# Summing the exponentials over the keys with products by a column of ones in an encoder block on one core

## The chip, the cores and the metric

The kernel runs on one core of a Trainium2 chip. The metric is the device time of one execution in microseconds. TensorE is called PE in the profile (PEld is its weight load), VectorE is DVE, ScalarE is ACT, GpSimd is POOL and SyncE is SP.

## What is computed

One layer of an encoder over 2064 tokens (16 meta tokens ahead of 2048) of width 1024, all in float32: an input projection, attention of four query heads over two key and value heads beside a Fourier mixing, an output projection, and a feed-forward part with a squared relu. The part that the change touches is the attention:

```python
def attend(qb):
    s = jnp.einsum('bkgqd,bksd->bkgqs', qb, kt).astype(jnp.float32) * scale
    p = jax.nn.softmax(s, axis=-1).astype(vt.dtype)
    return jnp.einsum('bkgqs,bksd->bkgqd', p, vt)
```

The softmax needs, for every query, the largest score and the sum of the exponentials over all 2064 keys.

## The kernel before

Most products of matrices are made three times on halves of a float32 number that `split` makes (a rounded high part on ACT by line 68, the rest on DVE by line 69), by `mm3` (lines 78 to 80).

The attention works in 16 units: eight blocks of 256 tokens by two key heads. A unit has 512 columns, two query heads of 256 tokens each, and keys lie on the partitions. `scores` (line 736) makes the scores of 128 keys by 512 queries, ACT copies them out of PSUM (line 754), and DVE keeps a running maximum `M` over tiles of keys (line 760). `stats` (line 780) then makes one maximum per query of what is left on 128 partitions, spreads it over all partitions and copies it to `mb`. `softmax` (line 786) subtracts `mb` (DVE, line 813), takes exponentials (ACT, line 814), adds them to `acc` (DVE, line 820) and multiplies them with the values into `O`. At its end `sum` (lines 799 to 801) holds 128 partial sums for each of the 512 queries, one per partition. `finish` (line 832) adds these up over the partitions, takes the reciprocal `rl` (line 837), spreads it over the partitions by four transposes (`rows_to_cols`, line 773, product `pd_l` on line 777), and DVE multiplies `O` with it (line 840).

The step over the partitions is `over_keys` (line 764), used for the maximum and for the sum: four transposes of 128 by 128 into a PSUM bank `pm`, and one reduction on DVE from that bank into `mx`. `pm` and the bank `pd` of `rows_to_cols` share one PSUM bank: `misc` (line 681) has one buffer. So the sequence around the end of a unit is a chain through that bank: `pm_m` (PE), `mx_m` (DVE), `pd_m` (PE), `mb` (ACT) for the next unit's maximum, then `pm_l` (PE), `mx_l` (DVE), `rl` (DVE), `pd_l` (PE) for the sum of the unit that ends.

The scores of the next unit, the softmax of this one and other work are issued step by step through generators: the end of the Fourier part, then `out_f` (line 879), then the output projection and the feed-forward part of the blocks whose attention is done. The order in which instructions end up on each engine is set by a scheduler, so a change in one step can move others. Two more places have a product by the column `ones` (line 176): line 904, one product per token tile (`pys`), and line 979, four products in a row per block (`pas`).

Of the kernel before, what the change touches and what calls it, by code (L numbers as in the profile page):

```python
# [11 lines left out]
F32 = mybir.dt.float32  # L12
R32 = mybir.dt.float32r
AF = mybir.ActivationFunctionType
ALU = mybir.AluOpType
AX = mybir.AxisListType
# [3 lines left out]
P = 128  # L20
# [34 lines left out]
def f32v(ap):  # L55
    return ap.bitcast(F32)
# [30 lines left out]
def bc(ap, shape):  # L87
    return ap.broadcast_to(shape)
# [45 lines left out]
def encoder_block(ctx: ExitStack, tc: tile.TileContext, x, meta, w_in, w_f,  # L134
                  w_out, w_up, w_down, g_fin, g_cols, g_rows, c_id, c_rope, c_dft, c_even, c_odd, c_rem, out):
    nc = tc.nc
    split = Split(nc)
    x = x[0]
# [37 lines left out]
    ones = const.tile([P, 1], F32, name="ones", tag="ones")  # L176
# [402 lines left out]
    for j in range(LAST + 1):  # L579
# [16 lines left out]
        else:  # L596
# [14 lines left out]
            a = 0  # L611
# [67 lines left out]
    ap2 = Lines(tc.alloc_tile_pool(name="ap2", bufs=1, side="right", reuse_waits="tile"), small)  # L679

    def misc(name, shape=(P, 512)):
        return app.tile(list(shape), F32, name=name, tag="misc")
# [35 lines left out]
    def attention():  # L718
# [42 lines left out]
            if i == NT - 1:  # L761
                nc.vector.tensor_tensor(M[:, 0], M[:, 0], M[:, 1], op=ALU.max)

        def over_keys(x, name, op):

            ps = misc("pm_" + name, (P, 4, P))
            for a in range(4):
                nc.tensor.transpose(ps[:, a], x[:, a * P:(a + 1) * P], ident)
            r = ap2.tile([P, 4], F32, name="mx_" + name, tag="mx", bufs=2)
            nc.vector.tensor_reduce(r, ps, axis=AX.X, op=op)  # L770
            return r

        def rows_to_cols(vec, name):

            ps = misc("pd_" + name, (P, 4, P))
            for a in range(4):
                nc.tensor.transpose(ps[:, a], bc(vec[:, a:a + 1], [P, P]), ident)
            return ps.rearrange("p a e -> p (a e)")

        def stats(u):  # L780
            s = state[u]
            pd = rows_to_cols(over_keys(s["M"], f"m{u}", ALU.max), f"m{u}")
            mb = s["mb"] = ap2.tile([P, 512], F32, name=f"mb_{u}", tag="mb", bufs=1)
            nc.scalar.copy(mb, pd)  # L784

# [46 lines left out]
        def finish(u):  # L832
            b, g = units[u]
            s = state.pop(u)
            sl = over_keys(s["sum"], f"l{u}", ALU.add)
            rl = ap2.tile([P, 4], F32, name=f"rl_{u}", tag="rl", bufs=2)
            nc.vector.reciprocal(rl, sl)
            O = ap2.tile([P, 512], F32, name=f"O_{u}", tag="Osb", bufs=1)
            nc.scalar.copy(O, s["O"])
            nc.vector.tensor_tensor(O, O, rows_to_cols(rl, f"l{u}"), op=ALU.mult)  # L840
            c = slice(b % 2 * 256, b % 2 * 256 + 256)
            hi = ap2.tile([P, 512], R32, name=f"oh_{u}", tag="ph", bufs=2)
            lo = ap2.tile([P, 512], R32, name=f"ol_{u}", tag="pl", bufs=2)
            split(hi, lo, O)
            for e, t in enumerate((hi, lo)):
                nc.sync.dma_start(o_d[b // 2][:, e, 2 * g:2 * g + 2, c], f32v(t).rearrange("p (h n) -> p h n", h=2))
            nc.scalar.square(O, O)
            first = b not in sqs
            if first:
                sqs[b] = ap2.tile([P, 256], F32, name=f"sq_{b}", tag="sq", bufs=3)  # L850
                nc.vector.tensor_tensor(sqs[b], O[:, :256], O[:, 256:], op=ALU.add)
            else:
                for h in range(2):
                    nc.vector.tensor_tensor(sqs[b], sqs[b], O[:, h * 256:(h + 1) * 256], op=ALU.add)

        start(0)
        for i in range(NT + 1):
            scores(0, i)
        yield
        stats(0)  # L860
        for u in range(len(units)):
            nx = u + 1 < len(units)
            for i in range(NT + 1 + LAG):
                if i == 1 and nx:
                    start(u + 1)
                if i <= NT:
                    softmax(u, i)
                if nx and i >= LAG:
                    scores(u + 1, i - LAG)
                yield  # L870
            if nx:
                stats(u + 1)
            finish(u)
            yield
# [41 lines left out]
    class Att:  # L916
        def __init__(self):
            self.gen = attention()
            self.n = 0
            self.cap = 1 << 30  # L920
# [372 lines left out]
    sl = Lines(tc.alloc_tile_pool(name="sl", bufs=1, reuse_waits="tile"), small)  # L1293
# [46 lines left out]
    for g in range(8):  # L1340
# [5 lines left out]
        for name in ORDER:  # L1346
            hi, lo = ready.pop(0)
            m = BF[name]
            for p in range(2):
# [5 lines left out]
                ps = slice(p * P, (p + 1) * P)  # L1355
# [10 lines left out]
            for p in range(2):  # L1366
# [12 lines left out]
                else:  # L1379
                    q, a, b = {"2": ("11", Y, p1), "7": ("22", X, p5), "3": ("12", Y, u2)}[name]  # L1380
# [315 lines left out]
```

## Time and profile before

| | |
|---|---|
| median of 3 runs | 2306.72 us (2306.57 to 2309.46) |
| profiled execution, its own time | 2308.2 us |
| its span | 2306.4 us |
| PE busy | 2277.9 us (99%) |
| PE weight loads | 1879.5 us (81%) |
| DVE busy | 1713.4 us (74%) |
| ACT busy | 1295.7 us (56%) |
| granted clock of PE | 1.00 |

Busy time of PE counts from the start of a product to the modelled end of its results, and neighbouring products overlap; so the cost of a product in a full stream is read from the distance between starts. Times in the timeline are from the start of the span. A row "x4" merges four neighbouring instructions.

### The profile page before, as it was taken

To read this page: it belongs to the slowest core of one execution; us is meant where nothing else is said; L and a number is where in the kernel's file an instruction comes from. 1 tells how busy PE (TensorE), PEld (TensorE's weight loads), DVE (VectorE), ACT (ScalarE), POOL (GpSimd) and SP (SyncE) were. 2 spreads that over 40 slices of the span, in tenths; PEclk is the share of its full clock that TensorE was granted. 3 is DMA by queue.
4 is the path that set the end of the run, shared out by engine and by line. 5 is a ranking of instruction groups with operands and counts; after the bars stand their busy time and mean duration, and the time that the engine had idled before them with its cause. 6 is when DMAs were issued, how large, how long until landed. Compare 5 with 4: busy or idle time off the path is not lost.

```text
span 2306.4 us, 29992 instructions
## 1 busy us (share of the span) xinstructions
PE 2277.9 (99%) x10822; PEld 1879.5 (81%) x10822; DVE 1713.4 (74%) x2435; ACT 1295.7 (56%) x2335; POOL 204.2 (9%) x243
## 2 busy tenths in 40 slices
PE   8999999999999999999999999999999999999998
PEld 7888987777788888888878878888888888888887
DVE  6445578999887876976887976886675646697786
ACT  6443355666675665665775675664555555543344
POOL 1212120233100000000000100000100000200000
PEclk9999999999999999999999999999999999999999
DMA  6343252543533322343242453325344444855442
GB/s 209 101 119 97 83 154 74 174 147 114 192 102 100 103 87 78 110 121 106 97 161 68 151 189 106 98 80 187 120 156 171 149 161 147 311 193 165 129 137 83
DMA packets 178069, 307.23 MB, mean 133 GB/s; under 512 B 14960, under 2 KB 63728, under 8 KB 177536
## 3 DMA queue, kind: packets, MB, share of 16 engines
q1 hardware_dynamic: 159280, 263.16, 34.8%
q0 software_dynamic: 18640, 42.16, 6.1%
q8 instruction: 85, 1.39, 0.2%
q14 instruction: 64, 0.52, 0.1%
HBM read 225.27 MB, written 79.99 MB: 132 GB/s over the span
## 4 chain that ended last, share of the span: by engine, by line
PE 73%; DVE 1%; ACT 1%; issue 1%; POOL 0%; DMA 0%; POOLq 0%; DVEq 0%; ACTq 0%; SPq 0%
PE pdn L78 5%; PE pdn L79 5%; PE pdn L80 5%; PE pup L78 5%; PE pup L80 5%; PE pup L79 5%; PE dx L80 2%; PE dx L79 2%; PE dx L78 2%; PE ux L78 2%; PE ux L79 2%; PE ux L80 2%; PE o L78 2%; PE o L79 2%; PE o L80 2%; PE dy L80 2%
## 5 line engine op out<-in xcount | busy, mean ns | idle before, releaser
L78 PE MATMUL pup<-mT,wh_up 128*128 128x512 f32 x512 | 200.8, 393 | 0.7 <-ACT mT L71 0.7
L80 PE MATMUL pup<-mT,wl_up 128*128 128x512 f32 x512 | 200.8, 393 | 0.3 <-DVE wl_up L69 0.3
L79 PE MATMUL pup<-mT,wh_up 128*128 128x512 f32 x512 | 200.7, 392 | 0.0
L79 PE MATMUL pdn<-wl_dn,ah 128*128 128x512 f32 x512 | 200.5, 392 | 0.0
L78 PE MATMUL pdn<-wh_dn,ah 128*128 128x512 f32 x512 | 200.4, 393 | 0.0
L80 PE MATMUL pdn<-wh_dn,al 128*128 128x512 f32 x512 | 199.2, 391 | 0.0
L754 ACT COPY S<-s 128x512 f32<-128x512 f32 x256 | 148.8, 584 | 46.1 <-PE s L80 36.9
L68 ACT CAST wh_up<-wr_up 128x512 fp32r<-128x512 f32 x128 | 79.3, 621 | 159.2 <-PE pup L79 79.2
L813 DVE TENSOR_TENSOR S<-S,mb 128x1024 f32<-128x1024 f32 x128 | 156.6, 1233 | 10.0 <-ACT mb L784 9.9
L69 DVE TENSOR_TENSOR pl<-S,ph 128x512 fp32r<-128x512 f32 x196 | 133.6, 700 | 11.5 <-ACT ph L68 10.9
L69 DVE TENSOR_TENSOR wl_up<-wr_up,wh_up 128x512 fp32r<-128x512 f32 x128 | 87.4, 688 | 68.1 <-ACT wh_up L68 63.1
L814 ACT ACTIVATE S<-S 128x1024 f32<-128x1024 f32 x114 | 120.4, 1058 | 30.2 <-DVE S L813 29.9
L68 ACT CAST ph<-S 128x512 fp32r<-128x512 f32 x196 | 119.9, 621 | 30.7 <-PE o L80 26.9
L820 DVE TENSOR_TENSOR acc<-acc,S 128x1024 f32<-128x1024 f32 x110 | 134.9, 1226 | 0.8 <-ACT S L814 0.5
L68 ACT CAST wh_dn<-wr_dn 128x512 fp32r<-128x512 f32 x128 | 78.9, 619 | 98.0 <-PE pdn L80 47.3
L760 DVE TENSOR_TENSOR M<-M,S 128x1024 f32<-128x1024 f32 x96 | 118.3, 1233 | 15.9 <-ACT S L754 15.0
L69 DVE TENSOR_TENSOR wl_dn<-wr_dn,wh_dn 128x512 fp32r<-128x512 f32 x128 | 87.3, 689 | 51.2 <-ACT wh_dn L68 43.9
L68 ACT CAST ah<-a 128x1024 fp32r<-128x1024 f32 x56 | 58.5, 1048 | 117.7 <-issue 60.8
L78 PE MATMUL s<-q,kt 128*128 128x512 f32 (+1 forms) x272 | 113.2, 416 | 2.9 <-ACT S L754 1.8
L78 PEld LDWEIGHTS pdn<-wh_dn,ah 128*128 128x128 f32 x512 | 96.1, 188 | 22.3 <-ACT r L1088 1.9
L78 PEld LDWEIGHTS pup<-mT,wh_up 128*128 128x128 f32 x512 | 96.2, 188 | 20.3 <-ACT mT L71 0.9
L80 PEld LDWEIGHTS pup<-mT,wl_up 128*128 128x128 f32 x512 | 96.2, 188 | 19.9 <-DVE wl_up L69 0.8
(336 smaller groups left out, 6434.1 us busy)
## 6 DMA issues: line engine op xcount, KB each, us to landing
wr_up<-in_w_up_dram SPq DMA_DIRECT2D x128, 256.0 KB, 2.8
wr_dn<-in_w_down_dram SPq DMA_DIRECT2D x128, 256.0 KB, 2.6
a<-s_d SPq DMA_DIRECT2D x42, 512.0 KB, 3.7
R<-in_w_up_dram SPq DMA_DIRECT2D x16, 1024.0 KB, 5.3
s_d<-s SPq DMA_DIRECT2D x64, 256.0 KB, 2.1
d<-in_w_down_dram SPq DMA_DIRECT2D x26, 512.0 KB, 5.0
s_d<-c SPq DMA_DIRECT2D x48, 256.0 KB, 2.0
x<-in_x_dram SPq DMA_DIRECT2D x16, 512.0 KB, 4.8
```

The source lines that it names most:

```text
L68: self.high = nc.scalar.copy(hi, src)
L69: self.low = nc.vector.tensor_tensor(lo, src, f32v(hi), op=ALU.subtract)
L78: nc.tensor.matmul(out, a[0], b[0], start=first, stop=False, skip_group_check=chain)
L79: nc.tensor.matmul(out, a[0], b[1], start=False, stop=False, skip_group_check=chain)
L80: nc.tensor.matmul(out, a[1], b[0], start=False, stop=last, skip_group_check=chain)
L754: nc.scalar.copy(S[:, i % 2], ps)
L760: nc.vector.tensor_tensor(M, M, S, op=ALU.max)
L813: nc.vector.tensor_tensor(S, S, mb, op=ALU.subtract)
L814: nc.scalar.activation(p, S, AF.Exp, scale=ISQ)
L820: nc.vector.tensor_tensor(acc, acc, p, op=ALU.add)
```

## The change

The sum over the partitions is taken out of the shared helper. The helper keeps the maximum, with one buffer of `mx` in place of two. The sum is made by four products of PE: a block of 128 partitions by 128 queries of `sum` with the column of ones, each giving one column of a PSUM tile of 128 by 4. No reduction follows: the reciprocal reads the PSUM tile. Lines from 775 on have a number that is higher by 7 (the reciprocal, line 837, is line 844; `pd_l`, line 777, is line 784).

```diff
-        def over_keys(x, name, op):
+        def most_over_keys(x, name):
             ps = misc("pm_" + name, (P, 4, P))
             for a in range(4):
                 nc.tensor.transpose(ps[:, a], x[:, a * P:(a + 1) * P], ident)
-            r = ap2.tile([P, 4], F32, name="mx_" + name, tag="mx", bufs=2)
-            nc.vector.tensor_reduce(r, ps, axis=AX.X, op=op)
+            r = ap2.tile([P, 4], F32, name="mx_" + name, tag="mx", bufs=1)
+            nc.vector.tensor_reduce(r, ps, axis=AX.X, op=ALU.max)
             return r
+
+        def sum_over_keys(x, name):
+            ps = misc("pm_" + name, (P, 4))
+            for a in range(4):
+                nc.tensor.matmul(ps[:, a:a + 1], x[:, a * P:(a + 1) * P], ones, start=True, stop=True)
+            return ps
...
-            pd = rows_to_cols(over_keys(s["M"], f"m{u}", ALU.max), f"m{u}")
+            pd = rows_to_cols(most_over_keys(s["M"], f"m{u}"), f"m{u}")
...
-            sl = over_keys(s["sum"], f"l{u}", ALU.add)
+            sl = sum_over_keys(s["sum"], f"l{u}")
             rl = ap2.tile([P, 4], F32, name=f"rl_{u}", tag="rl", bufs=2)
             nc.vector.reciprocal(rl, sl)
```

Where it moves instructions is shown at three places. The first is PE at the end of unit 6 (units count from 0; `pup` are products of the feed-forward part), before:

```order
L768 MATMUL pm_l_8324<-ident,sum_8224 128x128 x4
L80 MATMUL pup_3_3_8241<-mT_0_6452,wl_up_3_3_8353 128x512
L78 MATMUL pup_3_0_8238<-mT_0_6452,wh_up_3_4_8374 128x512
L79 MATMUL pup_3_0_8238<-mT_0_6453,wh_up_3_4_8374 128x512
L80 MATMUL pup_3_0_8238<-mT_0_6452,wl_up_3_4_8375 128x512
L78 MATMUL pup_3_1_8239<-mT_0_6452,wh_up_3_4_8374 128x512
L79 MATMUL pup_3_1_8239<-mT_0_6453,wh_up_3_4_8374 128x512
L80 MATMUL pup_3_1_8239<-mT_0_6452,wl_up_3_4_8375 128x512
L78 MATMUL pup_3_2_8240<-mT_0_6452,wh_up_3_4_8374 128x512
L79 MATMUL pup_3_2_8240<-mT_0_6453,wh_up_3_4_8374 128x512
L777 MATMUL pd_l_8335<-ident,rl_8331 128x128 x4
```

The same place of PE in the changed kernel:

```order
L777 MATMUL pm_l_8312<-ones,sum_8212 128x1 x4
L80 MATMUL pup_3_3_8229<-mT_0_6444,wl_up_3_3_8339 128x512
L78 MATMUL pup_3_0_8226<-mT_0_6444,wh_up_3_4_8360 128x512
L79 MATMUL pup_3_0_8226<-mT_0_6445,wh_up_3_4_8360 128x512
L80 MATMUL pup_3_0_8226<-mT_0_6444,wl_up_3_4_8361 128x512
L78 MATMUL pup_3_1_8227<-mT_0_6444,wh_up_3_4_8360 128x512
L784 MATMUL pd_l_8321<-ident,rl_8317 128x128 x4
```

The spreading transposes `pd_l` stood nine products behind `pm_l` and stand five behind it now. Over the 16 units the distance was 8 to 13 products and is 2 to 9; it is three in units 1, 11 and 13, two in the last, and five or more in the others.

The second place is DVE at the end of the same unit, before:

```order
L770 TENSOR_REDUCE mx_m_8315<-pm_m_8310 128x4
L813 TENSOR_TENSOR S_0_7686<-S_0_7686,mb_8322 128x1024
L770 TENSOR_REDUCE mx_l_8329<-pm_l_8324 128x4
L69 TENSOR_TENSOR wl_up_3_7_8433<-wr_up_3_7_8430,wh_up_3_7_8432 128x512
L837 RECIPROCAL rl_8331<-mx_l_8329 128x4
L813 TENSOR_TENSOR S_2_7758<-S_2_7758,mb_8322 128x1024
```

DVE there in the changed kernel:

```order
L770 TENSOR_REDUCE mx_m_8303<-pm_m_8298 128x4
L820 TENSOR_TENSOR S_0_7674<-S_0_7674,mb_8310 128x1024
L844 RECIPROCAL rl_8317<-pm_l_8312 128x4
L69 TENSOR_TENSOR wl_up_3_7_8419<-wr_up_3_7_8416,wh_up_3_7_8418 128x512
L820 TENSOR_TENSOR S_2_7746<-S_2_7746,mb_8310 128x1024
```

The reduction is gone, and the reciprocal stands in its place, right behind the first subtraction of the next unit.

The third place is DVE at the end of unit 11 in the changed kernel (`h` are sums of the feed-forward part):

```order
L770 TENSOR_REDUCE mx_m_12337<-pm_m_12332 128x4
L69 TENSOR_TENSOR wl_dn_1_1_2_12463<-wr_dn_1_1_2_12460,wh_dn_1_1_2_12462 128x512
L1121 TENSOR_TENSOR h_0_9318<-h_0_9318,pdn_1_0_0_12260 128x512
L1121 TENSOR_TENSOR h_1_9320<-h_1_9320,pdn_1_0_1_12261 128x512
L844 RECIPROCAL rl_12351<-pm_l_12346 128x4
L820 TENSOR_TENSOR S_0_11684<-S_0_11684,mb_12344 128x1024
```

Here, and in units 1 and 13, the reciprocal stands ahead of the first subtraction of the next unit; before, the subtraction stood ahead of `mx_l` in all units but the last.

## Rows read from the trace of the kernel before

**Rows 1.** The page, busy time of each engine.

```profile
PE 2277.9 (99%) x10822; PEld 1879.5 (81%) x10822; DVE 1713.4 (74%) x2435; ACT 1295.7 (56%) x2335; POOL 204.2 (9%) x243
```

**Rows 2.** Stretches of the attention: busy us (and instructions) of each engine, granted clock.

```profile
403.00:581.00 178.00, 171.94 (x785) 132.49 (x784) 167.93 (x235) 108.71 (x205) 56.75 (x54) 1.00 0.44 145
581.00:665.00 84.00, 82.54 (x388) 66.70 (x387) 67.67 (x100) 56.02 (x105) 10.54 (x12) 1.00 0.49 158
665.00:1600.00 935.00, 934.43 (x4216) 762.65 (x4215) 743.39 (x1024) 596.08 (x1018) 35.02 (x46) 1.00 0.36 113
```

**Rows 3.** Who waited for whom on PE: us in total, times, longest.

```profile
PE o L79 <- DVE pl L69: 3.5, 5, 1.6
PE s L78 <- ACT S L754: 1.8, 2, 1.5
...
PE pof L80 <- DVE yl L69: 1.0, 3, 0.4
```

**Rows 4.** Timeline of PE at the end of unit 6: start, us.

```profile
837.39 0.40 PE L79 MATMUL pup<-mT,wh_up 128*128 128x512 f32 x1
837.63 0.60 PE L768 MATMUL pm_l<-ident,sum 128*128 128x128 f32 x4
837.98 0.48 PE L80 MATMUL pup<-mT,wl_up 128*128 128x512 f32 x1
838.30 0.40 PE L78 MATMUL pup<-mT,wh_up 128*128 128x512 f32 x1
838.53 0.40 PE L79 MATMUL pup<-mT,wh_up 128*128 128x512 f32 x1
...
840.17 0.62 PE L777 MATMUL pd_l<-ident,rl 128*128 128x128 f32 x4
```

**Rows 5.** Groups by line and form on PE: count, busy us, mean ns.

```profile
L768 PE MATMUL pm_l<-ident,sum 128*128 128x128 f32 x64 | 9.8, 276 | 0.0
...
L979 PE MATMUL pas<-ones,sq 128*128 128x1 f32 x32 | 3.8, 239 | 0.0
```

**Rows 6.** Timeline of PE around the first four products with `ones` on line 979.

```profile
597.41 0.39 PE L80 MATMUL s<-q,kt 128*128 128x512 f32 x1
597.64 0.95 PE L979 MATMUL pas<-ones,sq 128*128 128x1 f32 x8
598.45 0.49 PE L78 MATMUL poa<-wh_oa,at 128*128 128x512 f32 x1
598.77 0.40 PE L79 MATMUL poa<-wl_oa,at 128*128 128x512 f32 x1
```

**Rows 7.** Timeline of PE around one product with `ones` on line 904.

```profile
588.45 0.28 PE L904 MATMUL pys<-ones,ysq 128*128 128x1 f32 x2
588.59 0.48 PE L80 MATMUL pof<-wfh,yl 128*128 128x512 f32 x1
```

**Rows 8.** Lines 770 and 837 on DVE: count, ns min/median/max.

```profile
L770 DVE TENSOR_REDUCE mx_l<-pm_l x16: 683/684/686, 405.1 to 1594.1; 128x4 f32<-128x512 f32 x16
...
L837 DVE RECIPROCAL rl<-mx_l x16: 169/172/179, 406.0 to 1594.8; 128x4 f32<-128x4 f32 x16
```

**Rows 9.** Timeline of DVE at the end of unit 6.

```profile
837.51 1.23 DVE L813 TENSOR_TENSOR S<-S,mb 128x1024 f32<-128x1024 f32 x1 [1.39 <-ACT mb L784]
838.65 0.68 DVE L770 TENSOR_REDUCE mx_l<-pm_l 128x4 f32<-128x512 f32 x1
839.25 0.68 DVE L69 TENSOR_TENSOR wl_up<-wr_up,wh_up 128x512 fp32r<-128x512 f32 x1
839.85 0.17 DVE L837 RECIPROCAL rl<-mx_l 128x4 f32<-128x4 f32 x1
```

## The prediction

> **What bounds the kernel now.** I read the page first: PE is busy for 99% of the span, DVE for 74% [rows 1]. An average says little about the places that the change touches, so I cut the attention into stretches next [rows 2]. From 665 to 1600 us, where 12 of the 16 units end, PE is busy for 934.43 of 935 us: it idles for 0.6 us, and DVE has a fifth of its time free. There the time is the sum of what PE issues. From 403 to 581 us it looks different: PE idles for 178.00 - 171.94 = 6.1 us and DVE is busy for 167.93 of 178 us, 94%. The view of waits names the work behind those idle spells: products with the exponentials that wait for the low half `pl` from DVE (3.5 us in five waits), scores that wait for ACT (1.8 us), and products of `out_f` that wait for `yl` from DVE (1.0 us) [rows 3]. So one stretch with three unit ends is partly held by DVE, and the rest by PE alone. The granted clock is 1.00 in each of them [rows 2].
>
> **What is taken away on PE.** Four transposes per unit, 64 in all [rows 5]. Their duration of 276 ns is no price, since products overlap; I take distances of starts. At the end of unit 6, from the product that starts at 837.39 to the one at 838.30 is 0.91 us, and that holds two products of 512 columns and the four transposes. A product of 512 columns takes 0.23 us from start to start (838.30 to 838.53). So the four transposes cost 0.91 - 0.46 = 0.45 us of PE's stream [rows 4].
>
> **What is added on PE.** Four products with one column each. The kernel already has just that: line 979 makes four such products in a row with the same column of ones and the same kind of stationary block. They appear as eight records [rows 6], 32 for the 16 products of the kernel [rows 5], so each float32 product leaves two. From 597.41 to 598.77 us is 1.36 us, with two products of 512 columns in it: 1.36 - 0.46 = 0.90 us for the four [rows 6]. The bound from below is the single product on line 904: its two records stand 0.14 us ahead of the next start, which would be 0.56 us for four, if nothing shifted the product behind them [rows 7]; from above, 0.95 us, the whole length of the eight records [rows 6]. I take 0.90, since it is the same group of four. The sum on PE is 0.90 - 0.45 = +0.45 us per unit, +7.2 us for 16. That one column of output costs more than 128 is no contradiction: what lies between starts here is two passes with a new stationary block each and nothing long to cover it.
>
> The Trainium skill, "Perfetto Trace Analysis", section "Identifying the Most-Contended Engine", holds that busy time of products is no measure of headroom and that the share of weight loads is a better one. By that share, 81%, PE would have room and the new products could be free, with a change near zero. The distances of starts do not agree: 0.23 us per product with 0.6 us of idle time in 935, so I keep the sum.
>
> **What is taken away on DVE.** The reduction, 684 ns in each of 16 units, 10.9 us [rows 8]. Between 581 and 1600 us it lies beside PE's stream, and what PE issues sets the time: worth nothing there. In the stretch from 403 to 581 us three units end, at its head and twice within it, each ahead of waits for DVE. For those three ends the change is worth between +0.45 us (PE sets the time) and -0.68 us (DVE does, and PE's added 0.45 only shortens a wait). I take zero for each of the three, near the middle, as DVE is not full and the waits are scattered.
>
> **What is moved.** The reciprocal now reads PSUM and stands where the reduction stood; the transposes `pd_l` come 2 to 9 products after the sums in place of 8 to 13. Does PE wait there? In unit 6 the sums would be done 0.95 us after their start at 837.63, at 838.58 [rows 4, 6]. DVE is then still in the subtraction, and the reduction started at 838.65 [rows 9]; the reciprocal can start then and end 0.17 us later, 838.82. PE reaches `pd_l` after the 0.90 us of the products and five products of 0.23, at 839.68. That leaves 0.86 us. With three products between, 0.46 us less: still 0.4; with two, 0.17 us. Before, `pd_l` started 0.15 us after the reciprocal's end (839.85 + 0.17 to 840.17), so even the last unit just fits. I cost the move at zero; the cover is those products, and if it is gone each unit pays its own wait. In three units the reciprocal stands ahead of the next unit's subtraction, which then waits for the sums, up to 0.95 us. DVE has the time for that in units 11 and 13, and it reaches PE only if the value products behind it have no slack; I count nothing, and 2.9 us at the worst for the three. One buffer of `mx` instead of two costs nothing: the one that is reused was read a whole unit earlier. The rest of the order on PE, SP and POOL shifts by a few places around these ends and in `out_f`; I count no sign for that, but it gives the range its width.
>
> **The sum.** 13 unit ends at +0.45 are +5.9 us, three at zero. The profiled execution took 2308.2 us, so its own time would be 2314.1. It lies 1.5 us above the median of the three runs, 2306.72; against the median the forecast is 2312.6 us. About 0.2%, 4.6 us, is what a measurement of this kernel can tell from no change, so this is slower by a little more than can be told.
>
> **The rivals.**
>
> *The idle time takes it up.* The shifted order and a DVE with less to do let all 6.1 us of PE's idle time from 403 to 581 us vanish. Then the change is 7.2 - 6.1 = +1.1 us, 2307.8 us: not slower in a measurement. It decides from 2.6 us of the 6.1 on. For it: DVE is named in two of the three waits. Against: DVE is 94% busy in that stretch, and three reductions are only 2.1 us.
>
> *PE waits for the reciprocal.* `pd_l` stands close behind the sums now, and whatever is late on DVE by one subtraction of 1.23 us [rows 9] outlasts the 0.86 us of cover by 0.37. In all 16 units that adds 5.9 us: 2318.5 us. For it: the distances have shrunk by about a half, and PE takes what stands in its order. Against: DVE has a fifth of its time free where most units end.
>
> *Each sum is made in four passes.* Then a group would leave 16 records, 1.80 us by the rows of line 979, +1.35 per unit, 17.6 us for the 13 ends: 2324.3 us. The Trainium skill, "FP8 and Floating Point Precision", section "Matmul Precision", says that true float32 takes four passes. The trace has two records for each such product (32 for 16), so this gets almost no chance, and the two passes are in the price that I use.
>
> *The products are cheaper than their model.* If they cost the lower bound of 0.56 us, the change on PE is only +1.8 us, and with PE's idle time from 403 to 665 us gone as well, 6.1 and 1.5 us [rows 2], it ends 5.8 us below the median, 2300.9 us. It is the only way to something faster that I can see, and both of its parts have to come true.
>
> **How the numbers follow.** The forecast gets 0.58, the rivals in this order 0.21, 0.12, 0.01 and 0.08. Of the forecast's 0.58, 0.13 falls short of 4.6 us, since the three ends in the stretch held by DVE may give back up to 2.0 us (5.9 - 2.0 = 3.9). Slower: 0.45 + 0.12 + 0.01 = 0.58. Within 0.2%: 0.13, 0.21 of the first rival and 0.02 of the last, 0.36. Faster: 0.06 of the last. The range begins at 2307.0, just under the first rival's time, and ends at 2316.5, which takes in all 16 ends at +0.45 (2313.9) and nearly half of the waits of the second rival.
>
> **What would show it.** After the change, line 777 should have 128 records of `pm_l` with one column, and the distance over each group, less two products, should be 0.90 us. PE's idle time from 665 to 1600 us should stay under 1 us, and DVE's busy time should fall by about 11 us with no gain behind it. The first rival shows as idle time of PE from 403 to 581 us well under 6 us, the second as a wait of `pd_l` for `rl` in the view of waits. I am wrong if the group costs no more than the transposes did, or if PE's idle time outside the groups changes by several us.

## The result and the profile after

The changed kernel takes 2318.1 us (median of 6 runs, 2317.14 to 2320.64) beside 2307.38 us for the kernel before in the same session (6 runs, 2306.57 to 2309.46): a ratio of 1.0046, 95% interval 1.0036 to 1.0056. That is slower, as forecast, but by 10.7 us where 5.9 were expected, and 1.6 us above the upper end of the range. The profiled execution took 2320.64 us, the slowest of the six, with a span of 2318.8 us.

The page, busy time of each engine, of the changed kernel:

```profile
PE 2286.3 (99%) x10886; PEld 1889.9 (82%) x10886; DVE 1706.5 (74%) x2419; ACT 1295.5 (56%) x2335; POOL 200.5 (9%) x243
```

PE has 64 records more than in [rows 1]: 128 of one column for 64 transposes. The groups by line and form on PE (count, busy us, mean ns, idle before) say the same:

```profile
L777 PE MATMUL pm_l<-ones,sum 128*128 128x1 f32 x128 | 15.8, 245 | 0.0
...
L784 PE MATMUL pd_l<-ident,rl 128*128 128x128 f32 x64 | 9.6, 272 | 0.0
```

And the end of unit 6 on PE, to be read beside [rows 4]:

```profile
840.90 0.40 PE L79 MATMUL pup<-mT,wh_up 128*128 128x512 f32 x1
841.13 0.97 PE L777 MATMUL pm_l<-ones,sum 128*128 128x1 f32 x8
841.97 0.48 PE L80 MATMUL pup<-mT,wl_up 128*128 128x512 f32 x1
842.29 0.39 PE L78 MATMUL pup<-mT,wh_up 128*128 128x512 f32 x1
...
843.20 0.60 PE L784 MATMUL pd_l<-ident,rl 128*128 128x128 f32 x4
```

From 840.90 to 842.29 us is 1.39 us with two wide products of 0.23 us in it: 0.93 us for the group, as in the kernel's other place of that kind [rows 6]. Measured in this way over all units, the 16 groups cost 15.4 us and the old transposes 7.7 us. `pd_l` does not wait for `rl`, and its 16 groups cost 7.1 us where they had cost 8.4. So, by these distances, the edit itself adds 7.7 - 1.3 = 6.4 us to PE's stream, 0.40 us per unit.

The rest of the 10.7 us stands in the stretches. Same columns as [rows 2], cut to where the difference lies; the kernel before:

```profile
403.00:456.00 53.00, 51.11 (x243) 37.29 (x242) 50.92 (x71) 32.20 (x57) 13.74 (x16) 1.00 0.53 165
...
1600.00:1645.00 45.00, 45.00 (x205) 37.25 (x204) 34.03 (x55) 22.21 (x41) 3.96 (x5) 1.00 0.52 172
```

The changed kernel:

```profile
403.00:456.00 53.00, 49.27 (x225) 35.65 (x226) 47.93 (x66) 31.56 (x55) 13.26 (x16) 0.97 0.49 150
...
665.00:1600.00 935.00, 933.76 (x4237) 764.48 (x4236) 734.08 (x1004) 589.53 (x1006) 34.62 (x46) 1.00 0.35 111
1600.00:1645.00 45.00, 43.39 (x195) 35.80 (x194) 31.61 (x49) 23.16 (x41) 2.59 (x1) 0.96 0.55 176
```

In 53 us at the head of the attention PE gets through 225 records instead of 243, although each group of sums has four more, and in 45 us behind its end 195 instead of 205. In both PE idles more, and in both the granted clock is below 1.00. Who waited for whom is in the view of waits (us in total, times, longest), here its rows of the whole kernel from the second to the sixth:

```profile
PE pys L911 <- POOL ysq L910: 2.5, 1, 2.5
PE o L78 <- ACT ph L68: 1.6, 4, 0.6
PE poa L78 <- ACT wh_oa L71: 1.6, 1, 1.6
PE o L79 <- DVE pl L69: 1.3, 2, 0.8
PE pm_m L768 <- DVE M L749: 1.2, 1, 1.2
```

None of the first, third and fifth is in [rows 3] or among the kernel's waits before, and none of them is at the sums. The waits that [rows 3] shows have shrunk: `o` for `pl` from 3.5 to 1.3 us, and that of `s` for ACT is gone from the list. The largest new one, on PE's timeline of the changed kernel:

```profile
435.22 0.39 PE L78 MATMUL pof<-wfh,yh 128*128 128x512 f32 x1
438.15 0.38 PE L911 MATMUL pys<-ones,ysq 128*128 128x1 f32 x2 [2.54 <-POOL ysq L910]
438.40 0.48 PE L79 MATMUL pof<-wfl,yh 128*128 128x512 f32 x1
438.71 2.92 PE L830 MATMUL o<-S,vn 128*128 128x512 f32 x4
...
441.85 0.63 PE L79 MATMUL s<-q,kt 128*128 128x512 f32 x1
442.28 0.63 PE L80 MATMUL s<-q,kt 128*128 128x512 f32 x1
```

This `pys` is the kernel's first, and its place on PE has hardly moved (one product of `out_f` now stands ahead of it). What has moved is on ACT. The squares `ysq` of that tile come in two pieces, and POOL adds when it has both. Before, the second piece followed the first:

```profile
422.11 0.44 ACT L900 ACTIVATE ysq<-EV 128x256 f32<-128x256 f32 x1
...
423.28 0.43 ACT L900 ACTIVATE ysq<-EV 128x256 f32<-128x256 f32 x1
```

```profile
426.29 2.16 POOL L903 TENSOR_TENSOR ysq<-ysq 128x256 f32<-128x256 f32 x2
```

POOL was done by 428.45 us (426.29 + 2.16), and `pys` came at 437.40, 9 us later. In the changed kernel's order fourteen instructions of ACT, evictions of scores, exponentials and casts of weights, stand between the two pieces:

```profile
434.25 0.45 ACT L907 ACTIVATE ysq<-EV 128x256 f32<-128x256 f32 x1
```

```profile
434.79 3.31 POOL L910 TENSOR_TENSOR ysq<-ysq 128x256 f32<-128x256 f32 x2 [3.00 <-ACT ysq L907]
```

POOL starts at 434.79 and ends at 438.10, and PE, which is at `pys` at 435.6, waits for it. (POOL takes 3.31 us for the two additions in this execution and took 2.16 before; the other profiles in this order show waits of 1.4 to 2.1 us here.) Behind the 2.54 us the products `s` start 0.43 us apart in place of 0.23: the lower of the two clock levels, 1.2 GHz, for 3.4 us. That is some 2.5 + 1.7 us in this place, less the 1.5 us that PE had waited for `S` of ACT at 436.6 us in the kernel before [rows 3].

The other place has its cause far from PE. On SP the second load of `R` (the next weights of the feed-forward part) was issued together with the first, ahead of the loads of `at`:

```profile
1591.75 0.93 SPq L1201 DMA_DIRECT2D R<-in_w_up_dram  x2
...
1602.74 1.85 SPq L988 DMA_DIRECT2D at<-o_d  x4
```

In the changed kernel it has fallen behind the loads of `at` and the first `wr_oa`:

```profile
1608.18 1.96 SPq L995 DMA_DIRECT2D at<-o_d  x4
...
1612.39 0.33 SPq L939 DMA_DIRECT2D wr_oa<-in_w_out_dram  x1
1612.82 0.38 SPq L1208 DMA_DIRECT2D R<-in_w_up_dram  x1
```

On ACT the cast of `R` stands ahead of the casts `wh_oa`, so ACT waits 4.82 us for the load, and PE's `poa` waits for ACT behind that (the 1.6 us above, at 1629 us):

```profile
1621.50 1.05 ACT L68 CAST wuh<-R 128x1024 fp32r<-128x1024 f32 x1 [4.82 <-DMA R<-in_w_up_dram]
1622.46 1.33 ACT L71 ACTIVATE wh_oa<-wr_oa,cols 128x512 fp32r<-128x512 f32 x2
```

So there are two theories to tell apart. **The first**: the time is the sum of two terms, the price of the products (0.9 us per group) and the price of the order that the scheduler made around them, which has nothing to do with the sums. **The rival**: the longer groups themselves push PE past what it used to meet, and the waits follow wherever they stand.

### The profile page after: what moved, and what is told of

It is laid out like the page before. It is cut to its first block, busy times and chain, and to the rows that moved or that the text cites. A ratio compares the mean times of both kernels' runs of the same rounds, so it can differ in the third digit from the quotient of the medians.

```text
span 2318.8 us, 30069 instructions
## 1 busy us (share of the span) xinstructions
PE 2286.3 (99%) x10886; PEld 1889.9 (82%) x10886; DVE 1706.5 (74%) x2419; ACT 1295.5 (56%) x2335; POOL 200.5 (9%) x243
## 3 DMA queue, kind: packets, MB, share of 16 engines
q8 instruction: 85, 1.39, 0.2%
## 4 chain that ended last, share of the span: by engine, by line
PE 77%; DVE 3%; issue 2%; ACT 2%; DMA 2%; POOL 1%; SPq 0%; POOLq 0%; DVEq 0%; ACTq 0%
PE pdn L78 5%; PE pdn L80 5%; PE pdn L79 5%; PE pup L80 5%; PE pup L78 5%; PE pup L79 5%; PE dx L80 2%; PE dx L79 2%; PE dx L78 2%; PE ux L78 2%; PE ux L79 2%; PE ux L80 2%; PE s L78 2%; PE s L80 2%; PE s L79 2%
## 5 line engine op out<-in xcount | busy, mean ns | idle before, releaser
L820 DVE TENSOR_TENSOR S<-S,mb 128x1024 f32<-128x1024 f32 x128 | 154.6, 1217 | 10.8 <-ACT mb L791 10.7
```

The source lines that it names most:

```text
L820: nc.vector.tensor_tensor(S, S, mb, op=ALU.subtract)
```

## The experiments

In several of these the order is fixed by hand. Behind the program a helper adds, on each engine, an edge from every instruction to the one that shall follow it; the edges carry no semaphore. In the traces every engine then issues in the sequence that was asked for:

```diff
         encoder_block(tc, *args)
+        _in_order(tc, ORDERS)
```

`ORDERS` is one sequence per engine. The edges themselves cost nothing that can be seen: the kernel below that keeps the changed kernel's own order up to 1575 us by such edges takes 8.45 us more than the kernel before from the sums of unit 0 to those of unit 14, and the changed kernel without edges 8.43 us (one spell at half clock in each). "The order of before" is the kernel before's own sequence, with the 16 reductions left out where the kernel has none.

**The new products in the old order, and the old in the new.** The first takes the changed kernel and gives every engine the order of before.

> The changed kernel's instructions in the order of the kernel before on all five engines (the 16 reductions left out). Theory 'two bills' (the products cost PE 0.92 us per unit where the transposes cost 0.45, 7.6 us in all, and the new order costs the rest, some 3 us): between 2312.5 and 2315.5 us, with no wait of a product with ones for POOL and none of the output projection for its weights. Rival 'all in the products' (they and the waits that they bring cost the whole 10.7 us): 2317 to 2318.5. Rival 'all in the order' (the products are hidden): 2307 to 2309.

Measured: 2313.81 us (2312.83 to 2314.59), ratio 1.0025 (1.0015 to 1.0035), 5.95 us above the kernel before in its session. PE's waits are those of [rows 3] again, but for `s`, which waits 0.3 us for ACT and not 1.8:

```profile
PE o L79 <- DVE pl L69: 3.6, 5, 1.6
PE s L78 <- DMA q<-q_d: 1.1, 1, 1.1
PE pof L80 <- DVE yl L69: 1.1, 3, 0.4
```

The second takes the kernel before, with transposes and reductions, and gives it the changed kernel's order; each reduction stands directly ahead of its reciprocal.

> The instructions of the kernel before (transposes and reductions) in the order of the changed kernel on all five engines, each reduction placed directly ahead of its reciprocal. 'Two bills': the order alone costs 2.5 to 4.5 us over the kernel before, 2310 to 2312, with the waits for POOL near 435 us and for the weights of the last output projection near 1627 us in the trace. 'All in the products': 2307 to 2309. 'All in the order': 2316 to 2318.

Measured: 2317.99 us (2317.26 to 2318.38), ratio 1.0043 (1.0030 to 1.0056). More than expected, and for a reason that the view of waits names:

```profile
PE pd_l L777 <- DVE rl L837: 4.0, 11, 0.6
...
PE pys L904 <- POOL ysq L903: 1.4, 1, 1.4
```

In the new order `pd_l` stands close behind `pm_l`, and with the reduction still in between PE waits 4.0 us for `rl` over 11 units. That is the rival of the prediction in which PE waits for the reciprocal; it needs the reduction to come true. The other 6 us are the order, with no new product in the kernel, and the wait of `pys` is among them. What follows from the pair: the products cost what was forecast, and the order costs about 4.3 us on top (2318.1 - 2313.8; 4.8 if each is taken against the kernel before in its own session). It costs something where no product has changed as well, though not the same: 6 us, and 4.0 more through the reduction.

**One queue at a time.** The changed kernel with only SP, or only POOL, in the order of before.

> The changed kernel with the order of the kernel before on SP alone, all other engines as in the changed kernel. 'Two bills': the wait of the last block's output projection for its weights goes, and with it the stretch at half clock behind it: 3 to 4 us less than the changed kernel, 2314 to 2315. If that wait is covered by something else or comes from ACT's order, no change: 2317 to 2318.5.

Measured: 2333.23 us (2331.40 to 2335.42), ratio 1.0110. It went the wrong way: the wait of `poa` for `wh_oa` at the end is gone, but a new one of 9.1 us appeared, with the clock at 0.87 from 1340 to 1380 us. Behind it stands ACT, which waits for a load of weights: SP in its old sequence issues it at 1355.49 us, and in the changed kernel at 1348.82. The next step of the maximum `M` on DVE waits for ACT in turn:

```profile
PE pm_m L768 <- DVE M L749: 10.3, 2, 9.1
```

```profile
1365.46 0.62 ACT L68 CAST wh_up<-wr_up 128x512 fp32r<-128x512 f32 x1 [12.13 <-DMA wr_up<-in_w_up_dram]
```

> The changed kernel with the order of the kernel before on POOL alone, all other engines as in the changed kernel. 'Two bills': the wait of the first product with ones of the output part for POOL near 435 us (2.5 us) shrinks and there is no stretch at half clock behind it: 1 to 3 us less than the changed kernel, 2315 to 2317. If POOL's order is not its cause (ACT hands over late), no change: 2317 to 2318.5.

Measured: 2320.49 us (2318.97 to 2323.65), ratio 1.0058; `pys` still waits for POOL, 1.7 us. So POOL's sequence is not the cause of that wait: the late piece on ACT holds it up whatever POOL does. The order is a set of five sequences that fit each other: with one of the old set among four new ones the kernel was 15 us slower in the case of SP, and with POOL 2.4 us, which the spread of the executions does not tell from nothing. The sequence of ACT, at which the wait of `pys` points, was not put back alone, nor were those of PE and DVE.

**Where in time the order costs.** All five sequences are spliced at a point where both orders have issued the same instructions: old up to about 640 us and new behind it, then new up to about 1575 us and old behind it.

> The changed kernel; up to about 640 us every engine issues in the order of the kernel before, behind that in the order of the changed kernel. Theory (the cost above 5.9 us is the new order, and some 3 us of it lie in the first third, with PE's wait for ysq of 2.5 us at 438 us and 3.4 us at half clock behind it): 2315.0 us, the wait for ysq gone, unit 3's sums within 0.5 us of where they stood before, the wait of poa for wh_oa at the end still there. Rival (the new products push DVE and PE past each other wherever they stand, whatever the order): 2318 us, and another wait of some 2 us in the first third.

Measured: 2315.49 us (2314.30 to 2317.01), ratio 1.0033 (1.0020 to 1.0045). The stretch from 403 to 456 us is whole again:

```profile
403.00:456.00 53.00, 52.09 (x248) 37.84 (x247) 50.68 (x71) 32.84 (x57) 14.53 (x16) 1.00 0.53 168
```

The wait of `pys` is gone and 2.6 us with it; the slowest of the five executions lies below the fastest of the changed kernel. Two parts missed: the sums of unit 3 stood 0.7 us late, not under 0.5, and the wait at the end was gone as well, though the order there was the new one.

> The changed kernel in its own order, and from about 1575 us on in the order of the kernel before on every engine. Theory (the late load of R puts the casts of wh_oa late, 1.6 us of waiting and 3.4 us at half clock; some 3.8 us in all lie in the tail): 2314.3 us, no wait of poa over 1 us and no half clock at 1630 us. Rival (the tail is late because what stands ahead of it is late): 2318 us.

Measured: 2316.91 us (2316.35 to 2319.86), ratio 1.0040 (1.0027 to 1.0052). The mechanism is there, PE busy for 45.00 of 45 us behind the attention's end, but the gain is 1.2 us and not 3.8, and the executions overlap with those of the changed kernel (2317.14 to 2320.64), so it is not clear of noise:

```profile
1600.00:1645.00 45.00, 45.00 (x209) 37.24 (x208) 32.38 (x50) 24.26 (x42) 1.46 (x1) 1.00 0.57 191
```

I had read the 3.8 us from the profiled execution, which lies 2.5 us above its own median; its granted clock was 0.998 and that of the other five executions 0.999, so they had less time at half clock. The two gains do not add up to a share of the 4.3 us, as the first splice had taken the wait at the end away too. What is shown is that a good half of the price comes and goes with the order up to 640 us; how the rest is spread over waits such as `o` for `ph` and `pm_m` for `M` is not.

**What makes up the price.** The changed kernel with `sum` and `ones` in the reduced float32 format of the score products, and two columns of ones in place of one, in the order of before. The sums are rounded to that format.

```diff
-                sm = s["sum"] = ap2.tile([P, 512], F32, ...)
+                sm = s["sum"] = ap2.tile([P, 512], R32, ...)
...
-                nc.tensor.matmul(ps[:, a:a + 1], x[:, a * P:(a + 1) * P], ones, ...)
+                nc.tensor.matmul(ps[:, a], x[:, a * P:(a + 1) * P], bc(ones, [P, 2]).bitcast(R32), ...)
```

> [...] Theory (a float32 product with one column is two passes, each with a stationary block of its own, and that is the price of 0.90 us per group): 64 records in place of 128, a group about 0.45 us, 2313.8 - 13 x 0.45 = 2308 us. Rival (the price is one of the product, so much for each whatever its passes): 0.90 us per group, 2313.8 us.

Measured: 2307.87 us (2306.67 to 2310.54, 11 runs), ratio 1.0001 (0.9992 to 1.0010), 5.94 us less than with the float32 products in the same order. The group, in the form of the table above:

```profile
L777 PE MATMUL pm_l<-ones,sum 128*128 128x2 f32 x64 | 8.6, 238 | 0.0
```

64 records for 128, and 0.48 us per group by the distances of starts, for 0.92. So the price goes with the records, some 0.12 us for each in both kernels, and not with the products. The one buffer of `mx` costs nothing either: this kernel has it. The same sums as the scheduler itself orders them, which is the changed kernel's order but for 12 instructions, give the order's price a second time, with cheap products:

> The sums in one pass as in e7, now in the order that the changed kernel has (12 of some 16,000 instructions stand elsewhere). Theory (the price of the products and the price of the order are two terms that add): 2307.9 + (2318.1 - 2313.8) = 2312.2 us, with the waits of PE that the changed kernel has. Rival (the waits of that order come from the products' length, which pushes PE behind what it used to meet): 2308 us.

Measured: 2313.59 us (2308.20 to 2315.74, 11 runs), ratio 1.0024 (1.0016 to 1.0033). The old waits of the new order are back without the long groups, and the order is worth 5.7 us here beside 4.3 us with the float32 products. The eleven executions spread over 7.5 us, so the two figures are not told apart:

```profile
PE pys L911 <- POOL ysq L910: 1.4, 1, 1.4
...
PE poa L78 <- ACT wh_oa L71: 1.3, 1, 1.3
...
PE pm_m L768 <- DVE M L749: 1.2, 1, 1.2
```

The rival of the length is out: `pys`, `poa` and `pm_m` wait in this order whether a group takes 0.92, 0.48 or 0.45 us (`poa` for 1.6, 1.3 and 0.7 us). The kernels of both orders side by side, in us; the kernel before had medians from 2307.4 to 2308.0 in their sessions:

| | order of before | order of the change |
|---|---|---|
| sums by transposes and DVE | 2307.4 | 2318.0, of which 4.0 are waits for the reduction |
| sums in one pass | 2307.9 | 2313.6 |
| sums in float32 (the change) | 2313.8 | 2318.1 |

**Looking for something better than both.** If a product with one column is dear, one with 512 should be cheap: a block of ones as the stationary side gives every partition all sums, and `rl` and `pd_l` go.

```diff
-            ps = misc("pm_" + name, (P, 4))
-            for a in range(4):
-                nc.tensor.matmul(ps[:, a:a + 1], x[:, a * P:(a + 1) * P], ones, ...)
+            ps = misc("pm_" + name)
+            nc.tensor.matmul(ps, bc(ones, [P, P]).bitcast(R32), x, ...)
...
-            nc.vector.reciprocal(rl, sl)
+            nc.vector.reciprocal(sl, sl)
...
-            nc.vector.tensor_tensor(O, O, rows_to_cols(rl, f"l{u}"), op=ALU.mult)
+            nc.vector.tensor_tensor(O, O, sl, op=ALU.mult)
```

> One product per unit with a stationary block of ones (128 x 128) and the 512 columns of sums as the moving side, in the reduced float32 format (the sums are rounded to it): each partition gets all sums, DVE takes the reciprocal of 128x512 and multiplies; the four products, the reciprocal of 128x4 and the four transposes pd_l are gone. The order is that of the kernel before with these left out. Theory (PE's stream sets the time): per unit 0.23 us in place of 0.45 and 0.47 us, -0.69 us for 13 ends, -9.0 us from the kernel before: 2298.9 us. Rival (DVE's wider reciprocal, about 0.7 us or more per unit, holds PE from 403 to 581 us and where the sums' bank is held longer): 2303 us or more.

Measured: 2364.94 us (2361.04 to 2365.94), ratio 1.0245: the theory was off by 66 us. The groups of DVE by line and form show why:

```profile
L844 DVE RECIPROCAL pm_l<-pm_l 128x512 f32<-128x512 f32 x16 | 53.7, 3359 | 0.0
```

I had put the reciprocal near 0.7 us, like other operations of DVE on 128x512. It takes 3.36 us, and the next unit's subtractions queue behind it on DVE, the exponentials behind those on ACT, and PE waits for their high halves:

```profile
PE o L78 <- ACT ph L68: 18.2, 6, 3.7
```

PE is busy for 904.49 of 935 us from 665 to 1600 us, at a clock of 0.98.

So the reciprocal should stay at 128x4, and the spreading can be one product: DVE multiplies the identity by `rl`, and a block of ones adds the diagonal up.

```diff
+            D = ap2.tile([P, 512], R32, name="D_" + name, tag="pl", bufs=2)
+            nc.vector.tensor_tensor(D.rearrange("p (a e) -> p a e", a=4),
+                                    bc(ident.rearrange("p (o e) -> p o e", o=1), [P, 4, P]),
+                                    bc(vec.rearrange("p (a o) -> p a o", o=1), [P, 4, P]), op=ALU.mult)
+            nc.tensor.matmul(ps, bc(ones, [P, P]).bitcast(R32), D, start=True, stop=True)
-            for a in range(4):
-                nc.tensor.transpose(ps[:, a], bc(vec[:, a:a + 1], [P, P]), ident)
```

> e7 with another way to spread the reciprocals: DVE multiplies the identity by them (128x512, in the reduced float32 format, to which they are rounded) and one product with a block of ones takes the place of the four transposes pd_l. PE: 0.23 us for 0.47 per unit, DVE: 0.69 us more per unit, which is what the reduction had cost. Theory (PE's stream sets the time, DVE's addition is hidden where the reduction was): 2307.9 - 13 x 0.24 = 2304.8 us. Rival (pd_l waits for the longer chain on DVE): a wait of pd_l in the view of waits and 2308 us or more.

Measured: 2308.98 us (2307.69 to 2310.23, 11 runs), ratio 1.0005 (0.9996 to 1.0013), no gain. `D` takes 0.69 us on DVE as expected, but `pd_l`, which has cost 0.44 us in four transposes, costs 0.24 us only in 4 units and 0.37 to 1.13 us in the others: PE reaches it before DVE is done, and in all 12 of them it starts 0.15 us behind the end of `D`.

> e11 with the maxima spread in the same way (rounded to the reduced format, the same value for all keys of a query): another 0.24 us less on PE per unit and 0.69 us more on DVE, here in the chain that the next unit's exponentials wait for. Theory (PE's stream alone): 2304.8 - 3.1 = 2301.7 us. Rival (DVE's addition lies in the chain of the maxima, where DVE is nearly full from 403 to 581 us): 2305 us or more, with longer waits of PE for ph or pl there.

Measured: 2318.60 us (2316.74 to 2319.77), ratio 1.0046 (1.0032 to 1.0059). For the maxima the cover is shorter still, and the wait larger than the whole gain:

```profile
PE pd_m L787 <- DVE D_m L783: 9.3, 14, 0.9
```

> e11 with the product pd_l three products later on PE in every unit, nothing else moved. In e11 pd_l cost 0.24 us where it didn't wait for D (4 units) and 0.45 to 1.13 us in the others. Theory (the gain of e11 was lost to that wait): pd_l 0.24 us in nearly all units, 2307.9 - 13 x 0.21 = 2305.2 us. Rival (DVE's 0.69 us more per unit delays PE in other places too): 2307.5 us or more.

Measured: 2309.74 us (2308.39 to 2310.80, 11 runs), ratio 1.0008 (0.9999 to 1.0017). `pd_l` now costs 0.24 us in 12 of 16 units and 4.5 us in all, where the four transposes had cost 7.1, so the local theory holds, and the time does not fall: waits have grown elsewhere, `o` for `ph` to 1.8 us and `pof` for `yl` to 1.7 us, from 0.3 and 1.0 with the transposes. Where the rest of the 2.6 us went was not followed up. No version that was tried beats the kernel before.

## Why the prediction was right and wrong

**The price of the group was right.** 0.90 us was read from four products of the same kind elsewhere in the kernel [rows 6]; 15.4 us for 16 groups is 0.96 each, with a median of 0.92. It goes with the records: halving them halved it. The lower bound of 0.56 us in the last rival was read too short: in [rows 7] the product behind the single one is delayed as well. The Trainium skill, "FP8 and Floating Point Precision", section "Matmul Precision", has true float32 at four passes. The two records of each product, from which I gave that rival almost no chance, do not settle this: in the same trace the 32 float32 products of 512 columns on line 823 leave two records each as well, and these start 0.43 us apart, where one in the reduced format takes 0.23. What settles it here is the price: 0.92 us per group and not the rival's 1.80, and 2324.3 us was not reached.

**Three ends near zero was right; the agreement of the sum has luck in it.** In the profile of the new products in the old order the sums of unit 0 start 0.55 us earlier than before, with nothing changed ahead of them, and those of unit 3 start 0.16 us earlier. So the three ends between cost 0.4 us, where 0.40 for each would be 1.2; PE idles for 5.1 us from 403 to 581 us there and not 6.1. In the stretch partly held by DVE most of the longer groups was paid for by shorter waits. From unit 4 to unit 15 the distance grows by 3.8 us, 0.34 per unit where 0.45 was forecast. In that one profiled execution there is also a spell at half clock at 634 us, behind which PE stands 1.6 us later than before it; whether the timed ones had it cannot be told. The agreement of 5.95 with 5.9 us is thus better than the readings deserve.

**PE's bound was right.** The Trainium skill, "Perfetto Trace Analysis", section "Identifying the Most-Contended Engine", judges TensorE's headroom by the share of weight loads, beside that of the peak arithmetic; that share is 82% now and would leave room. The time followed PE's stream instead: two kernels with the same order, one with 0.44 us more per group, differ by 5.94 us.

**The move of `pd_l` was right at zero waits, and a little better.** No wait for `rl` is left: `pd_l` starts 0.84 us behind the end of the reciprocal in unit 6, 0.41 to 0.43 us with three products between and 0.20 us in the last unit, where 0.86, 0.4 and 0.17 were worked out. One reading was wrong. Before, `pd_l` starts 0.14 to 0.15 us behind the reciprocal's end in ten units, which I took for cover; in just these ten its four transposes cost 0.48 to 0.61 us and in the others 0.43 to 0.45. They had waited, too briefly for the view, and the 1.3 us that this cost are gone. That rival would have needed the reduction to stay (4.0 us in 11 units).

**The step that failed** is the sentence: "The rest of the order on PE, SP and POOL shifts by a few places around these ends and in `out_f`; I count no sign for that, but it gives the range its width." It put at nothing a term that had a sign and a size, 4.3 us, and the range was not widened by it: its ends came from the idle time and from the rival of the reciprocal. The sign of being wrong that the prediction named came true: PE idles for 32.5 us of the span where it had idled for 28.5. Of the 5.5 us between 2312.6 and 2318.1, another 0.7 are the kernel before, whose median of six is 2307.38 and not 2306.72. Nor was it a few places: between the two traces about 270 instructions of PE, 220 of DVE, 200 of ACT, 7 of POOL and 15 of SP have changed their place in the sequence. Two things could have been seen in the order. On ACT, which the sentence does not even name, the second piece of a square had fallen behind fourteen instructions, with POOL and PE waiting for it in turn. On SP a load of `R` had moved behind the loads of `at`, with its cast ahead of `wh_oa` on ACT. Each is a wait of PE with a name, and a direction: later. I had compared PE and DVE at the ends of units, where the change is, and not where the order had moved most.

Two smaller misses: PE idles for 1.2 us from 665 to 1600 us where under 1 was expected, and DVE's busy time fell by 6.9 us and not 11. The order does not explain this: it fell by 5.1 us with the new products in the old order and by 11.5 us in the one-pass kernel in the same order. Most of that spread lies ahead of the attention. In the first 300 us, where nothing was changed, DVE is busy for 154.7 us before, 156.0 in the changed kernel and in the one with the old order, and 151.9 in the one-pass kernel; from 300 us on it fell by 8.2, 6.4 and 8.6 us. A reduction also overlaps its neighbours a little, with 0.60 us from start to start where it takes 0.68 [rows 9].

## What to carry to other kernels

Where PE's stream is full, a float32 product with one output column costs as much here as one of 512 columns in the reduced format (0.23 us each), and twice a transpose of the same block (0.11 us): trading transposes and a reduction on an engine with room for such products moves work to the engine that has no room. A change of one step under a scheduler has two prices, that of its instructions and that of the order that comes out; fix the order of issue to the old one and the first can be measured alone. Before costing the second at zero, look at every queue, far from the edit as well, for a load, a cast or a product that has moved ahead of or behind the work that waits for it.

## What was not expected of the hardware

A reciprocal on DVE of 128x512 takes 3359 ns beside 172 ns for 128x4 [rows 8], some 6.3 ns for each column more, where a multiplication of 128x512 takes about 690 ns. (The wide one reads and writes PSUM; the changed kernel's reciprocal of 128x4, which reads PSUM too, takes 176 ns.)

The same stall can leave the clock alone or halve it. In the kernel before, PE at 630 us:

```profile
631.50 1.63 PE L1045 MATMUL pmt<-ident,m 128*128 128x128 f32 x8 [0.79 <-ACT m L1040]
...
634.84 0.39 PE L78 MATMUL s<-q,kt 128*128 128x512 f32 x1
635.07 0.39 PE L79 MATMUL s<-q,kt 128*128 128x512 f32 x1
```

And with the new products in the same order:

```profile
631.80 1.64 PE L1052 MATMUL pmt<-ident,m 128*128 128x128 f32 x8 [0.79 <-ACT m L1047]
...
635.79 0.63 PE L78 MATMUL s<-q,kt 128*128 128x512 f32 x1
636.22 0.63 PE L79 MATMUL s<-q,kt 128*128 128x512 f32 x1
```

A second wait of 0.67 us follows in both. The waits are the same to 0.01 us, and the products behind them are the same; in the second the starts are 0.43 us apart for 3.4 us, in the first 0.23. In the second trace PE is 0.30 us later than in the first ahead of this place and 1.87 us behind it, so the drop costs 1.6 us. All fourteen profiles of this case have these two waits, to 0.01 us; in five of them (the new products in the old order, both splices, the one-pass sums in the new order, and reciprocals and maxima both spread by a product) a spell of 3.4 us at half clock follows, and in nine none. So it cannot be forecast from the waits alone. Behind the waits of 2.5 and 1.6 us in the changed kernel there was one each in the profiled execution.
